# PEER layer: one-hot rows made on ScalarE, and all u blocks ahead of the first v block

## The chip, the cores and the metric

The kernel runs on one core of one Trainium2 chip. The metric is the device time of one execution in microseconds. Engines are named as the profile names them: PE is TensorE, DVE is VectorE, ACT is ScalarE, POOL is GpSimd, SP is SyncE, whose queue issues the loads.

## What is computed

The reference is a model of three layers over 256 tokens of width 1024. The change lies in one part of the first layer, a PEER layer: 16384 experts, laid out as 128 x 128, of which each token uses 8 x 16 = 128.

```
q = (xt @ w_q).reshape(BLOCK, PEER_HEADS, PEER_QDIM)
s1, s2 = q[..., :half] . keys1,  q[..., half:] . keys2
t1, i1 = top_k(s1, 16);  t2, i2 = top_k(s2, 16)
ts, sel = top_k(t1[:, None] + t2[None, :], 16)     # 16 of 256 pairs per head
idx = i1 * 128 + i2 of the pairs chosen
g = softmax(ts)
act = gelu(u[idx] . xt)
out = sum over chosen experts of (g * act) * v[idx]
```

The kernel gathers no rows of u or v. It computes GELU(u . x) for all 16384 experts and all 256 tokens, multiplies it with a matrix of coefficients that is g at the chosen experts and 0 elsewhere, and multiplies the product with all of v.

## The kernel before

Weights come as blocks of 128 x 1024 float32 (512 KB). For each block, SP issues a load into one of a few places (`prefetch`, L152), ACT makes the rounded upper part (L138), and DVE the remainder (L163, `losplits`); then the place is free for another load. `pump` runs this ahead of PE: the split on ACT is issued three blocks ahead of the block that PE works on, and DVE's part of a block one block later. The order on every engine is the order in which the program issues; nothing reorders it later. Waits between engines follow from tiles being written and read.

The experts are cut in 128 u blocks and 128 v blocks. A u block (`ublock`) is 24 matmuls of 256 columns (`lin_b`, L192 to L194), and its GELU is put into `ring`, which is 128 blocks x 256 tokens in SBUF. A v block (`row_a`, L204 to L208) is 12 matmuls of 512 columns that add into four PSUM banks.

The layer has three stretches. In the first, 66 u blocks are computed while DVE and POOL work out the top 16 (`unit`). The second builds the coefficients. `rT` holds, with heads and choices along the partitions and tokens along the columns, i1 (row 0), i2 (row 1) and g (row 2); it is filled by transposes on PE and ACT copies (L955). For every group of four tokens (64 groups, `group`) there are two factors per token, made by `onehots`: `e`, on POOL (L968), one-hot rows of i2, and `a`, on DVE (L970), one-hot rows of i1 times g. Four matmuls (L980, each two PE instructions) contract the two over the 128 choices, which gives the 128 x 128 coefficients of a token. For blocks whose GELU is already in the ring, DVE multiplies it by them (L983); for the others ACT stores the coefficients in the ring (L984), and the block's own GELU is multiplied in later (`ublock`, L901, L903, L905: columns of the tokens already built are handled apart from the rest). `e` has three buffers and `a` two; the one-hots of a group are issued one group ahead, inside the group before.

Beside the groups run u blocks: 26 of them, with `NU2 = 28` and two more ahead of the transposes. The loop issues one u block, then as many groups as keep the two lists in step:

```
for i in range(2, NU2):
    ublock(u)
    u += 1
    while g * (NU2 - 2) < NG * (i - 1):
        group(g, u)
        g += 1
```

In the third stretch the v blocks run. `coef` splits two ring blocks into upper part and remainder (L221, L222), one pair ahead. The 34 u blocks that are left are issued one behind each of the first 34 v blocks. `plan_peer` puts the loads in the same order. While the coefficients are built, three 512 KB places take incoming blocks: two of the base pool and the first half of `h`. The second half holds `rT` and becomes a fourth place when the stage ends; two pieces of the ring are added from v block 32 on.

Of the kernel before, what the change touches and what calls it, by code (L numbers as in the profile page):

```python
# [11 lines left out]
AF = mybir.ActivationFunctionType  # L12
OP = mybir.AluOpType
# [6 lines left out]
S = 256  # L20
# [5 lines left out]
NF = FF // 128  # L26
EXP_BLOCKS = 128
NU1 = 66
NU2 = 28
PACE = 1.7  # L30
QB = 6
BURST = 1.4
# [56 lines left out]
class Net:  # L89
# [665 lines left out]
    def plan_peer(self):  # L755
# [5 lines left out]
        for hd in range(8):  # L761
            p.append(A["peer_wq"][2 * hd])
            p.append(A["peer_wq"][2 * hd + 1])
            for _ in range(QB):
                p.append(A["peer_u"][u])
                u += 1
        while u < NU1 + NU2:
            p.append(A["peer_u"][u])
# [7 lines left out]
    def peer(self, h, dg, spool):  # L776
# [3 lines left out]
        nc, tc, A = self.nc, self.tc, self.A  # L780
        mm = nc.tensor.matmul
        with ExitStack() as ctx:
            one = ctx.enter_context(tc.tile_pool(name="p1", bufs=1))
            wctx = ctx.enter_context(ExitStack())
            ring = one.tile([128, EXP_BLOCKS, S], F32, name="ring")
# [26 lines left out]
            iota = self.c("iota")  # L812
# [73 lines left out]
            def ublock(b):  # L886

                n = 4 * built[0]
                if b < NU1 + 2:
                    if b % 2 == 0:  # L890
                        pair["p"] = self.ps.tile([128, 512], F32, name="b", tag="b")
                    p = pair["p"]
                    self.lin_b(p[:, (b % 2) * S:(b % 2 + 1) * S], self.chunk(), 0, x2T, KB, 0, S)
                    if b % 2 == 1:
                        nc.scalar.activation(ring[:, b - 1:b + 1, :].rearrange("p a b -> p (a b)"), p,
                                             AF.Gelu_apprx_tanh)
                    return
                p = self.bank(S)
                self.lin_b(p, self.chunk(), 0, x2T, KB, 0, S)
                if n:  # L900
                    nc.scalar.activation(p[:, :n], p[:, :n], AF.Gelu_apprx_tanh)  # L901
                if n < S:
                    nc.scalar.activation(ring[:, b, n:], p[:, n:], AF.Gelu_apprx_tanh)  # L903
                if n:
                    nc.vector.tensor_mul(out=ring[:, b, :n], in0=p[:, :n], in1=ring[:, b, :n])  # L905
# [44 lines left out]
            rT = h[:, 1, :768].rearrange("p (a b) -> p a b", b=S)  # L950
            for c0, n in ((0, 2), (2, 1)):
                p = self.ps.tile([128, 512], F32, name="acc", tag="acc")
                for i in range(2 * n):
                    nc.tensor.transpose(p[:, i * 128:(i + 1) * 128], res[:, c0 + i // 2, i % 2, :], self.ident)
                nc.scalar.activation(rT[:, c0:c0 + n, :].rearrange("p a b -> p (a b)"), p[:, :n * S], AF.Copy)  # L955

            used[1] = 0
            et = [carve((4, 128), F32, 1) for _ in range(3)]
# [3 lines left out]
            def onehots(g):  # L962
                if g >= NG:
                    return
                t0 = 4 * g
                e, a = et[g % 3], at[g % 2]
                for i in range(4):
                    nc.gpsimd.tensor_scalar(e[:, i, :], iota, rT[:, 1, t0 + i:t0 + i + 1], None, op0=OP.is_equal)  # L968
                for i in range(4):
                    nc.vector.tensor_scalar(a[:, i, :], iota, rT[:, 0, t0 + i:t0 + i + 1], rT[:, 2, t0 + i:t0 + i + 1],  # L970
                                            op0=OP.is_equal, op1=OP.mult)
                st[g] = (e, a)

            def group(g, nb):

                t0 = 4 * g
                e, a = st.pop(g)
                p = self.ps.tile([128, 512], F32, name="acc", tag="acc")
                for i in range(4):
                    mm(p[:, i * 128:(i + 1) * 128], e[:, i, :], a[:, i, :], start=True, stop=True)  # L980
                pg = p.rearrange("p (t b) -> p b t", b=128)
                onehots(g + 1)
                nc.vector.tensor_mul(out=ring[:, :nb, t0:t0 + 4], in0=pg[:, :nb, :], in1=ring[:, :nb, t0:t0 + 4])  # L983
                nc.scalar.activation(ring[:, nb:, t0:t0 + 4], pg[:, nb:, :], AF.Copy)  # L984
                built[0] = g + 1

            onehots(0)
            g = 0
            for i in range(2, NU2):
                ublock(u)  # L990
# [4 lines that stand above are left out]
# [36 lines left out]
            for i, w in enumerate(self.chunks(3)):  # L1031
                b = EXP_BLOCKS - 3 + i
# [516 lines left out]
```

## Time and profile before

Three runs took 2177.15, 2177.68 and 2179.26 us; the median is 2177.68. The profiled execution took 2177.61 us, its span is 2175.8 us.

| engine | busy us | share of the span | instructions |
|---|---|---|---|
| PE (matmul) | 2122.0 | 98% | 14386 |
| DVE | 1349.3 | 62% | 2458 |
| ACT | 1078.1 | 50% | 1720 |
| POOL | 309.7 | 14% | 436 |

The share of busy time is a mean over stretches with different limits. The chain that ended last is followed back from the last instruction; for each moment it names the work that everything behind it waited for. A row of the grouped instructions ends with the idle time of the engine just before them and what ended it. A PE instruction's time includes a tail that overlaps with the next one, so sums of PE's rows are longer than the time they cover, and starts are compared instead.

### The profile page before, as it was taken

The page shows a single profiled execution, that of the slowest core. Times are in us where ns is not written, and L with a number is a line of the kernel's source. Part 1 is how long each engine was busy: PE and PEld are TensorE (multiplying, and loading weights), DVE is VectorE, ACT ScalarE, POOL GpSimd, SP SyncE. Part 2 cuts the span into 40 slices and gives each one's busy share as a digit, 9 for nine tenths or more (in the row PEclk, how much of TensorE's full clock was granted, in tenths as well). Part 3 has the DMA queues.
Part 4 walks back from the last instruction along what each step waited for, and adds up shares of the span by engine and source line. Part 5 has one row for each costly group of instructions (what it writes and reads, how often), then busy time and mean ns, then how long its engine had stood idle before and what let it go on. Part 6 is the DMA issues. An engine that isn't in the chain of part 4 may idle for free.

```text
span 2175.8 us, 36723 instructions
## 1 busy us (share of the span) xinstructions
PE 2122.0 (98%) x14386; PEld 1914.6 (88%) x14386; DVE 1349.3 (62%) x2458; ACT 1078.1 (50%) x1720; POOL 309.7 (14%) x436
## 2 busy tenths in 40 slices
PE   8999999999998999999999999999999999999998
PEld 8987889999887889888888899887999999878997
DVE  6666669897777555555555554577554654586454
ACT  5666554444333444444445544586444544475443
POOL 1221111111999300000001000011000000010000
PEclk9999999999999999999999999999999999999999
DMA  6433455565222455555555655533555555534553
GB/s 220 144 109 107 147 176 178 181 185 175 88 79 78 148 189 196 188 187 186 193 188 170 226 183 195 166 107 130 196 179 191 168 179 197 176 98 157 198 179 117
DMA packets 99709, 356.40 MB, mean 164 GB/s; under 512 B 11040, under 2 KB 13344, under 8 KB 99280
## 3 DMA queue, kind: packets, MB, share of 16 engines
q1 hardware_dynamic: 98304, 349.58, 48.9%
q0 software_dynamic: 656, 3.41, 0.4%
q8 instruction: 114, 1.87, 0.3%
q10 hardware_dynamic: 576, 1.06, 0.1%
q14 instruction: 59, 0.48, 0.1%
HBM read 351.90 MB, written 2.10 MB: 163 GB/s over the span
## 4 chain that ended last, share of the span: by engine, by line
PE 82%; POOL 9%; DVE 5%; issue 2%; ACT 2%; DMA 0%; SPq 0%; POOLq 0%; DVEq 0%; ACTq 0%
PE b L192 15%; PE b L194 15%; PE b L193 15%; PE acc L204 10%; PE acc L206 10%; PE acc L208 10%; POOL work L968 8%; DVE wlo L163 2%; PE acc L235 1%; PE acc L237 1%; PE acc L236 1%; PE acc L299 1%; PE acc L676 0%; PE acc L677 0%; PE b L505 0%
## 5 line engine op out<-in xcount | busy, mean ns | idle before, releaser
L192 PE MATMUL b<-xhi,whi 128*128 128x256 f32 x2416 | 681.5, 282 | 2.7 <-issue 2.3
L194 PE MATMUL b<-xhi,wlo 128*128 128x256 f32 x2416 | 676.2, 280 | 2.0 <-DVE wlo L163 2.0
L193 PE MATMUL b<-xlo,whi 128*128 128x256 f32 x2416 | 676.0, 280 | 0.0
L163 DVE TENSOR_TENSOR wlo<-raw,whi 128x1024 fp32r<-128x1024 f32 x451 | 537.4, 1227 | 44.9 <-ACT whi L138 43.2
L138 ACT ACTIVATE whi<-raw 128x1024 fp32r<-128x1024 f32 x451 | 463.8, 1052 | 73.0 <-PE acc L208 43.6
L192 PEld LDWEIGHTS b<-xhi,whi 128*128 128x128 f32 x2416 | 456.0, 189 | 8.0 <-issue 2.5
L193 PEld LDWEIGHTS b<-xlo,whi 128*128 128x128 f32 x2416 | 455.9, 189 | 4.3
L194 PEld LDWEIGHTS b<-xhi,wlo 128*128 128x128 f32 x2416 | 455.8, 189 | 2.6 <-DVE wlo L163 2.6
L1101 DVE TENSOR_TENSOR silu<-silu,b 128x256 f32<-128x256 f32 x88 | 37.0, 421 | 300.9 <-PE b L194 292.4
L968 POOL TENSOR_SCALAR work<-cst,h 128x128 f32<-128x128 f32 x256 | 175.4, 706 | 23.1 <-ACT h L955 23.1
L138 ACT ACTIVATE whi<-ring 128x1024 fp32r<-128x1024 f32 x106 | 112.0, 1058 | 114.6 <-issue 43.3
L204 PE MATMUL acc<-whi,chi 128*128 128x512 f32 x500 | 157.9, 397 | 1.5 <-ACT chi L221 1.5
L206 PE MATMUL acc<-wlo,chi 128*128 128x512 f32 x500 | 157.3, 396 | 0.0
L208 PE MATMUL acc<-whi,clo 128*128 128x512 f32 x500 | 157.3, 397 | 0.0
L221 ACT ACTIVATE fhi<-silu 128x256 fp32r<-128x256 f32 x88 | 36.8, 418 | 240.8 <-DVE silu L1101 240.8
L163 DVE TENSOR_TENSOR wlo<-ring,whi 128x1024 fp32r<-128x1024 f32 x106 | 132.0, 1246 | 12.9 <-ACT whi L138 12.8
L163 DVE TENSOR_TENSOR wlo<-h,whi 128x1024 fp32r<-128x1024 f32 x103 | 126.9, 1232 | 7.6 <-ACT whi L138 7.6
L242 POOL TENSOR_SCALAR r<-ss 128x1 f32<-128x1 f32 x16 | 4.8, 298 | 864.4 <-ACT acc L269 672.6
L222 DVE TENSOR_TENSOR clo<-ring,chi 128x512 fp32r<-128x512 f32 x64 | 44.2, 693 | 120.8 <-ACT chi L221 118.9
L206 PEld LDWEIGHTS acc<-wlo,chi 128*128 128x128 f32 x500 | 94.3, 189 | 22.8
L208 PEld LDWEIGHTS acc<-whi,clo 128*128 128x128 f32 x500 | 94.2, 188 | 22.8
L192 PE MATMUL b<-ohi,whi 128*128 128x256 f32 x400 | 112.4, 281 | 0.0
(398 smaller groups left out, 3677.0 us busy)
## 6 DMA issues: line engine op xcount, KB each, us to landing
raw<-ffn_in SPq DMA_DIRECT2D x176, 512.0 KB, 4.1
raw<-ffn_out SPq DMA_DIRECT2D x88, 512.0 KB, 4.6
h<-peer_u SPq DMA_DIRECT2D x61, 512.0 KB, 4.5
ring<-peer_u SPq DMA_DIRECT2D x46, 512.0 KB, 3.7
ring<-peer_v SPq DMA_DIRECT2D x46, 512.0 KB, 3.5
h<-peer_v SPq DMA_DIRECT2D x42, 512.0 KB, 4.5
raw<-peer_v SPq DMA_DIRECT2D x40, 512.0 KB, 3.6
raw<-w_in SPq DMA_DIRECT2D x38, 512.0 KB, 4.1
```

Of the source, the lines that this page charges most:

```text
L138: nc.scalar.activation(t, self.raw[j], AF.Copy)
L163: self.nc.vector.tensor_sub(out=t, in0=self.raw.pop(j), in1=self.hi[j].bitcast(F32))
L192: mm(ps, whi[:, s], xhi[:, k, n0:n1], start=(k == 0), stop=False)
L193: mm(ps, whi[:, s], xlo[:, k, n0:n1], start=False, stop=False)
L194: mm(ps, wlo[:, s], xhi[:, k, n0:n1], start=False, stop=(k == nk - 1))
L204: mm(acc[tb * 2 + h], xhi[:, k, t], whi[:, h * 512:(h + 1) * 512], start=first, stop=False)
L206: mm(acc[tb * 2 + h], xhi[:, k, t], wlo[:, h * 512:(h + 1) * 512], start=False, stop=False)
L208: mm(acc[tb * 2 + h], xlo[:, k, t], whi[:, h * 512:(h + 1) * 512], start=False, stop=last)
L221: nc.scalar.activation(hi, src, AF.Copy)
L222: nc.vector.tensor_sub(out=lo, in0=src, in1=hi.bitcast(F32))
L968: nc.gpsimd.tensor_scalar(e[:, i, :], iota, rT[:, 1, t0 + i:t0 + i + 1], None, op0=OP.is_equal)
L1101: nc.vector.tensor_mul(out=s, in0=s, in1=pu)
```

## The change

`onehots` makes `e` on ACT. For each of four tokens one activation computes |column - i2|, with -i2 as the bias per partition, and one more over all four computes relu(1 - that). `rT` therefore holds -i2 in row 1, and its filling is three copies in place of two. `onehots` runs two groups ahead instead of one, with one more call before the loop. `NU2` is 62: 60 u blocks run beside the groups, and no u block is left for the v stretch. The ACT store behind the multiplication is left out where all blocks are already in the ring.

```diff
-NU2 = 28
+NU2 = 62
...
-                nc.scalar.activation(rT[:, c0:c0 + n, :].rearrange("p a b -> p (a b)"), p[:, :n * S], AF.Copy)
+                if c0 == 0:
+                    nc.scalar.activation(rT[:, 0, :], p[:, :S], AF.Copy)
+                    nc.scalar.activation(rT[:, 1, :], p[:, S:], AF.Copy, scale=-1.0)
+                else:
+                    nc.scalar.activation(rT[:, 2, :], p[:, :S], AF.Copy)
...
                 for i in range(4):
-                    nc.gpsimd.tensor_scalar(e[:, i, :], iota, rT[:, 1, t0 + i:t0 + i + 1], None, op0=OP.is_equal)
+                    nc.scalar.activation(e[:, i, :], iota, AF.Abs, bias=rT[:, 1, t0 + i:t0 + i + 1])
+                nc.scalar.activation(e, e, AF.Relu, scale=-1.0, bias=1.0)
...
-                onehots(g + 1)
+                onehots(g + 2)
                 nc.vector.tensor_mul(out=ring[:, :nb, t0:t0 + 4], in0=pg[:, :nb, :], in1=ring[:, :nb, t0:t0 + 4])
-                nc.scalar.activation(ring[:, nb:, t0:t0 + 4], pg[:, nb:, :], AF.Copy)
+                if nb < EXP_BLOCKS:
+                    nc.scalar.activation(ring[:, nb:, t0:t0 + 4], pg[:, nb:, :], AF.Copy)
                 built[0] = g + 1
 
             onehots(0)
+            onehots(1)
```

## Rows read from the trace of the kernel before

**Rows 1.** The page's fourth part: shares of the chain that ended last, by engine.
```profile
PE 82%; POOL 9%; DVE 5%; issue 2%; ACT 2%; DMA 0%; SPq 0%; POOLq 0%; DVEq 0%; ACTq 0%
```
**Rows 2.** Busy times by stretch: length, PE, PEld, DVE, ACT, POOL (instructions), clock, DMA.
```profile
304.00:514.00 210.00, 206.23 (x1746) 204.28 (x1747) 192.83 (x548) 98.56 (x121) 34.57 (x30) 1.00 0.59 180
549.00:726.20 177.20, 157.99 (x1131) 140.80 (x1129) 136.52 (x372) 60.07 (x143) 175.16 (x256) 0.99 0.27 84
726.20:1177.40 451.20, 451.20 (x2335) 381.78 (x2336) 242.75 (x262) 212.82 (x260) 1.67 (x3) 1.00 0.57 189
```
**Rows 3.** The chain inside 549 to 727 us: start, length, work.
```profile
548.80 163.97 POOL work L968 x240
```
**Rows 4.** Instructions grouped by line, 549 to 725 us: busy, mean ns, idle before.
```profile
L968 POOL TENSOR_SCALAR work<-cst,h 128x128 f32<-128x128 f32 x256 | 175.4, 706 | 23.1 <-ACT h L955 23.1
L980 PE MATMUL acc<-work 128*128 128x128 f32 x512 | 89.5, 301 | 17.7 <-DVE work L970 12.0 <-POOL work L968 2.5 <-ACT ring L984 0.2
...
L163 DVE TENSOR_TENSOR wlo<-raw,whi 128x1024 fp32r<-128x1024 f32 x17 | 20.8, 1224 | 0.0
```
**Rows 5.** PE in order of time, 547 to 727 us: start, length, instruction.
```profile
547.99 0.37 PE L192 MATMUL b<-xhi,whi 128*128 128x256 f32 x1
...
643.98 0.37 PE L192 MATMUL b<-xhi,whi 128*128 128x256 f32 x1
...
646.87 1.05 PE L980 MATMUL acc<-work 128*128 128x128 f32 x8
...
726.17 1.22 PE L204 MATMUL acc<-whi,chi 128*128 128x512 f32 x2 [1.48 <-ACT chi L221]
```
**Rows 6.** ACT's instructions grouped by line and shape, whole span.
```profile
L1314 ACT ACTIVATE z<-z,swmx 128x128 f32<-128x128 f32 x16 | 6.3, 395 | 11.2 <-DVE swmx L1312 11.1
...
L543 ACT ACTIVATE gel<-gel 128x512 f32<-128x512 f32 x1 | 0.6, 632 | 0.0
```
**Rows 7.** ACT in order of time, 1450 to 1454 us (a later layer).
```profile
1450.84 1.28 ACT L1161 ACT_TABLE_LOAD   x1
1452.14 0.53 ACT L1161 ACTIVATE e<-e 128x384 f32<-128x384 f32 x1
1452.57 0.48 ACT L1158 ACTIVATE e<-acc 128x384 f32<-128x384 f32 x1
1453.08 0.53 ACT L1161 ACTIVATE e<-e 128x384 f32<-128x384 f32 x1
```
**Rows 8.** ACT in order of time, 1464 to 1467 us.
```profile
1464.61 1.77 ACT L1167 ACTIVATE e<-e 128x384 f32<-128x384 f32 x4
1466.28 0.47 ACT L1158 ACTIVATE e<-acc 128x384 f32<-128x384 f32 x1
```
**Rows 9.** ACT and DVE in order of time, 633 to 638 us.
```profile
633.32 0.26 ACT L901 ACTIVATE b<-b 128x120 f32<-128x120 f32 x1 [0.35 <-PE b L194]
...
633.92 0.28 DVE L905 TENSOR_TENSOR ring<-b,ring 128x120 f32<-128x120 f32 x1 [1.13 <-ACT ring L903]
634.12 1.30 DVE L970 TENSOR_SCALAR work<-cst,h 128x128 f32<-128x128 f32 x4
635.34 0.48 DVE L983 TENSOR_TENSOR ring<-acc,ring 128x324 f32<-128x324 f32 x1
635.85 0.33 ACT L984 ACTIVATE ring<-acc 128x188 f32<-128x188 f32 x1 [1.96 <-DVE ring L983]
...
637.33 0.33 ACT L984 ACTIVATE ring<-acc 128x188 f32<-128x188 f32 x1 [1.15 <-DVE ring L983]
637.56 1.05 ACT L138 ACTIVATE whi<-raw 128x1024 fp32r<-128x1024 f32 x1
```
**Rows 10.** PE in order of time, 960 to 963 us, v blocks alone.
```profile
960.17 0.63 PE L204 MATMUL acc<-whi,chi 128*128 128x512 f32 x2
...
962.97 0.40 PE L204 MATMUL acc<-whi,chi 128*128 128x512 f32 x1
```
**Rows 11.** Loads, 726 to 960 us: count, size, median us to landing.
```profile
h<-peer_u SPq DMA_DIRECT2D x31, 512.0 KB, 4.6
```

## The prediction

> **What bounds the kernel now.** I read the page's chain that ended last first: PE holds 82% of it and POOL 9% [rows 1]. So there is a place where POOL, not PE, sets the pace. The busy times by stretch say where: in 549.0 to 726.2 us, the stage that builds the coefficients, POOL is busy 175.16 of 177.20 us, PE 157.99, DVE 136.52 and ACT only 60.07; in the stretch behind it, 726.2 to 1177.4, PE is busy for the whole 451.20 [rows 2]. The chain inside the stage is one piece: 163.97 us of POOL work of line 968 [rows 3]. The grouped instructions name it: 256 comparisons of 128x128, mean 706 ns, 4 to each of the 64 groups of tokens, and PE's matmuls of line 980 are the ones that stand idle before them [rows 4].
>
> How much of the stage PE needs is worked out from its starts. A u block starts at 643.98 and the group behind it at 646.87, so a block takes 2.89 us [rows 5]. A group is 8 PE instructions in 1.05 us, whose last, of about 0.275, overlaps with what follows: (1.05 - 0.275) / 7 = 0.11 from start to start, and 8 x 0.11 = 0.89 us [rows 5]. The stage lasts from the start of its first u block, 547.99, to the first v matmul, 726.17: 178.2 us [rows 5]. It holds 26 u blocks and 64 groups, 26 x 2.89 + 64 x 0.89 = 75.1 + 57.0 = 132.1. PE is therefore held up for 46.1 us, 1.48 of them at the end, where it waits for the first coefficients. That is what is to be had.
>
> **The change part by part.** *POOL's comparisons* go: 256 x 706 ns, and the pace of 2.7 us per group with them. Nothing else in the stage runs on POOL.
>
> *ACT's part.* Each group gets four Abs with a bias read per partition, and one Relu over 4 x 128. The nearest row for Abs is the exponential of 128x128 with such a bias, 395 ns; for Relu the 128x512 activation in place, 632 ns; its constant bias of 1.0 adds nothing visible: line 1167 has one too, and four of its instructions over 384 columns take 1.77 us, (1.77 + 3 x 0.10) / 4 = 0.52 each, as the 0.53 of line 1161 without one [rows 6, 7, 8]. Independent ACT instructions overlap by 0.10 us (1452.14 + 0.53 against the start at 1452.57), while one that reads the result of the one before starts 0.03 us after its end (1452.57 + 0.48, next at 1453.08) [rows 7]. So Abs and Relu take 3 x 0.295 + 0.395 + 0.03 + 0.632 = 1.94 us, 1.84 if the first overlaps too. If nothing overlaps it is 4 x 0.395 + 0.03 + 0.632 = 2.24; this is the upper bound, the lower is 1.84, and I take 1.84, since the rows of this engine with such a bias overlap as well.
>
> *The chain of one block.* ACT's order per block is: split of a weight block, GELU in two pieces, Abs and Relu for two groups ahead, and the copy of line 984, which waits for DVE's line 983. From the trace, with the two pieces of GELU starting at 633.32, line 905 starts at 633.92, line 970 at 634.12, line 983 at 635.34, the copy at 635.85: 2.53 us [rows 9]. ACT's own way to that point is about 0.57 of GELU and 1.84, 2.41, so the copy still waits for DVE, not for the new work. Line 983 grows from 4 x 69 to 4 x 128 columns; over its 324 columns in 0.48 us the mean of 394 is worth about 0.07 more. From the copy to the split is 0.23 us (637.33 to 637.56), on average about 0.17, since the copy shrinks to nothing; the split is 1.05, less 0.10 of overlap [rows 9]. One block: 2.53 + 0.07 + 0.17 + 0.95 = 3.72 us on ACT. Sixty blocks carry 64 groups, so four blocks have a second one, for which ACT needs 1.84 + 0.27 = 2.1: 60 x 3.72 + 4 x 2.1 = 231.6 us. PE needs 60 x 2.89 + 64 x 0.89 = 173.4 + 57.0 = 230.4 us. The two come out level. ACT, with 60.07 of 177.20 us busy, is the cover for this edit; after it there is none left.
>
> *What two level engines lose.* They wait for each other a little. The nearest stretch with a second engine almost full is 304 to 514, where DVE is busy 192.83 of 210.00 us and PE 206.23, a loss of 1.8% [rows 2]. I take 4 us of 232. Abs is issued two groups ahead (hence onehots(1) before the loop) and the splits three blocks ahead, so the four double blocks are absorbed rather than paid one by one. Before the loop ACT has 2 x 1.94 us of one-hots ahead of its first split, and the second group comes about 1 us late for PE; that is within the 4.
>
> *DVE.* The new wait is that the four comparisons of line 970 for group g+2 use the buffer that group g's matmuls read, so they wait for PE. Behind them in DVE's queue stands line 983 of group g, which waits for the same matmuls: what moves is its order, 1.1 us later, and that is in the chain above. Per block DVE has 1.22 for a remainder [rows 4], 0.28 for line 905 and 64/60 times the 1.7 from line 970's start to line 983's end [rows 9]: 3.3 us, under 3.8.
>
> *34 u blocks move* from among the v blocks into the stage, with their loads, splits, GELUs and multiplications; nothing of it is added or saved. A v block alone takes 2.80 us (960.17 to 962.97) [rows 10]. Behind the stage 128 x 2.80 = 358.4 us are left of 451.2, so 92.8 go and 34 x 2.89 = 98.3 come in the stage, already counted there. ACT's copy of the transposed indices becomes three instructions in place of two, 0.3 us once, at the head of ACT's queue. The scale of -1 costs nothing.
>
> *Loads.* SP's queue keeps its order. In the stage three 512 KB places hold incoming blocks, as before, but a block is wanted every 3.8 us in place of 6.8. From one split to the next split out of the same place there are 3 x 3.8 = 11.4 us; needed are one block until DVE's turn (3.8), its 1.22 [rows 4], and a landing, which took 4.6 us in the busier stretch behind the stage: 9.7 [rows 11]. Hidden, with 1.7 us to spare. In the v stretch four places give 4 x 2.8 = 11.2 against 2.8 + 1.22 + 4.6 = 8.6.
>
> **Sum.** Before: 178.2 + 92.8 = 271.0 us for what moves or changes. After: 230.4 + 4 + 1.5 (the same wait for the first coefficients) = 235.9. Gain 35.1. The profiled execution took 2177.61 us (span 2175.8), within 0.1 of the median 2177.68: 2177.6 - 35.1 = 2142.5, say 2143. Without any loss between ACT and PE it would be 231.9 and 2138.5; if a u block in the denser stage packed like 2.80 us, 5 less, 2133. That is the low end.
>
> **The rivals.**
>
> *ACT becomes the bound.* For: its sum is already 231.6. If nothing on it overlaps, a block takes 0.60 + 2.24 + 0.03 + 0.27 + 1.05 + 0.03 = 4.22 us and a second group 2.55: 60 x 4.22 + 4 x 2.55 + 1.5 = 264.9, a gain of 6, 2171.5. Against: the overlap in [rows 7], and DVE's waits, not ACT's work, end the copy's wait. Halfway, 4.0 us, gives 60 x 4.0 + 4 x 2.3 + 1.5 = 250.7, a gain of 20, 2157.
>
> *Loads come late.* If landing took 7 us in place of 4.6, the three places would set 12.0 / 3 = 4.0 us per block: 60 x 4.0 + 4 x 0.89 + 1.5 = 245, a gain of 26, 2152. Against: the landing in [rows 11].
>
> *Table loads; this is the slower side.* GELU, Abs and Relu run on one engine in turn. If Abs and Relu weren't served by the table that GELU has loaded, each block would load twice, and the row has 1.28 us for one, with the next instruction 0.02 us behind it [rows 7]. On a chain that has nothing to spare: 60 x (3.72 + 2.57) + 4 x 2.1 + 1.5 = 387, against 271: 116 slower, 2294. It decides from 0.63 us per block on, since 60 x 4.35 + 8.4 + 1.5 = 271. Against: line 1158's Abs runs right behind the logarithm of line 1167 with no load [rows 8], and it is the exponential of line 1161 that loads one; line 1158 at 1452.57 also follows an exponential without one [rows 7]. No row shows Relu, nor Abs behind GELU.
>
> The Trainium skill, "ScalarE: Activation LUTs", section "Table sets: the hidden batching unit", says that cheap functions such as relu and abs are filler in every set; by that rule the rival falls. The page's section "What ACT_TABLE_LOAD costs" speaks of about 1380 ns of drain on top of a 1283 ns load; by it the rival would be 60 x 2 x 1.38 = 166 us worse still. The trace has the 1283, and no such drain between its instructions.
>
> **How the numbers follow.** Likeliest, PE and ACT level: 0.65, own range 2134 to 2151. ACT bound, 2151 to 2172: 0.21. Loads, 2148 to 2160: 0.06. Table loads: 0.03. Something unseen that eats most of the gain, or more: 0.05. The range 2134 to 2164 leaves out about 2 in 10: the upper part of the second case and the last two. A measurement of this kernel tells some 0.2%, 4.4 us. Slower: 0.03 + 0.01 = 0.04; within 0.2%: 0.03; faster: 0.93.
>
> **What would show it.** POOL gone from the chain of the stage; the stage about 236 us long with 60 u blocks; PE's idle time there under 6 us; ACT over 90% busy in it; the four Abs starting about 0.30 us apart; the copy of line 984 still waiting for DVE; v blocks every 2.80 us behind it. It is wrong if ACT loads tables in the stage, if Abs starts 0.4 us apart, if PE waits for Relu block after block, or if the splits wait for loads.

## The result, and the profile after

Four runs of the changed kernel took 2129.17 to 2131.19 us, median 2129.88; the kernel before has 2177.41 over its four. The ratio is 0.9783, 95% interval 0.9771 to 0.9796: 2.2% faster. The sign and the mechanism are as forecast, but the gain is 47.5 us where 35 were forecast, and the time lies below the range. The profiled execution took 2129.37 us, its span is 2127.6.

The page's chain that ended last has lost POOL (9% in [rows 1]); PE has its share:

```profile
PE 91%; DVE 5%; ACT 2%; issue 1%; POOL 1%; DMA 0%; SPq 0%; POOLq 0%; DVEq 0%; ACTq 0%
```

Busy times by stretch, columns as in [rows 2]. The stage now runs from 547.3 to 776.2 us. In its middle PE is busy for all of 213.50 us and ACT for 203.57; POOL does nothing. What PE loses lies in the first and the last 8 us:

```profile
546.70:554.70 8.00, 7.34 (x62) 7.07 (x61) 6.17 (x20) 7.83 (x22) 0.00 (x0) 1.00 0.60 197
554.70:768.20 213.50, 213.50 (x1853) 213.50 (x1852) 169.52 (x411) 203.57 (x535) 0.00 (x0) 1.00 0.45 139
768.20:776.20 8.00, 5.66 (x51) 5.47 (x49) 6.17 (x13) 5.42 (x15) 0.00 (x0) 1.00 0.53 166
```

The waits of PE's matmuls in the stage (who waited for whom: us in total, times, longest). In [rows 4] matmuls of the groups stood idle for 17.7 us; now one of them waits, and the first v block waits for the first coefficients:

```profile
PE acc L204 <- ACT chi L221: 2.3, 1, 2.3
PE acc L986 <- ACT work L974: 0.7, 1, 0.7
```

PE in order of time, to set beside [rows 5] (the group is now line 986). From one group to the next are 3.70 us, 0.81 from the group's start to the u block and 2.89 back to a group:

```profile
641.73 1.05 PE L986 MATMUL acc<-work 128*128 128x128 f32 x8
642.54 0.36 PE L192 MATMUL b<-xhi,whi 128*128 128x256 f32 x1
...
645.43 1.05 PE L986 MATMUL acc<-work 128*128 128x128 f32 x8
```

ACT over the same block, to set beside [rows 9] (973 is Abs, 974 Relu, 991 the copy), with DVE's multiplication, line 989, that the copy waits for: no table load in it, Abs about 0.3 us apart, everything on ACT seemingly back to back:

```profile
641.93 0.24 ACT L901 ACTIVATE b<-b 128x104 f32<-128x104 f32 x1
642.20 0.30 ACT L903 ACTIVATE ring<-b 128x152 f32<-128x152 f32 x1
642.40 1.27 ACT L973 ACTIVATE work<-cst,h 128x128 f32<-128x128 f32 x4
643.70 0.64 ACT L974 ACTIVATE work<-work 128x512 f32<-128x512 f32 x1
643.74 0.54 DVE L989 TENSOR_TENSOR ring<-acc,ring 128x372 f32<-128x372 f32 x1
644.37 0.29 ACT L991 ACTIVATE ring<-acc 128x140 f32<-128x140 f32 x1
644.56 1.05 ACT L138 ACTIVATE whi<-raw 128x1024 fp32r<-128x1024 f32 x1
645.62 0.24 ACT L901 ACTIVATE b<-b 128x108 f32<-128x108 f32 x1
```

The copy starts 0.09 us after the multiplication ends (643.74 + 0.54 against 644.37). It does so, with the same 0.09, in every block with one group from 588 to 770 us: the copy still waits for DVE, as forecast. The view of waits lists only the later of these blocks, from 694 us on, where ACT was idle for 0.15 us or more; it puts 16 down to DVE and 6 to PE. The columns that DVE multiplies grow from block to block, so ACT's time from one GELU (line 901) to the next grows too, from 3.49 us early to 3.75 at the end:

```profile
763.65 0.36 ACT L901 ACTIVATE b<-b 128x240 f32<-128x240 f32 x1
...
765.61 0.67 DVE L989 TENSOR_TENSOR ring<-acc,ring 128x500 f32<-128x500 f32 x1
766.38 0.18 ACT L991 ACTIVATE ring<-acc 128x12 f32<-128x12 f32 x1 [0.32 <-DVE ring L989]
...
767.41 0.36 ACT L901 ACTIVATE b<-b 128x244 f32<-128x244 f32 x1
```

Where the 48 us of span went, from the starts of the first u block of the stage, the first v matmul, the last matmul of line 208, and the end:

| stretch | before | after | difference |
|---|---|---|---|
| ahead of the stage | 548.0 | 547.3 | -0.7 |
| the stage (26 or 60 u blocks, 64 groups) | 178.2 | 228.9 | +50.7 |
| v blocks (with 34 u blocks or none) | 446.6 | 349.9 | -96.7 |
| behind them | 1003.0 | 1001.5 | -1.5 |

The last row of the table has no cause in the change that I can show; all profiles below but two have 1001.5 to 1001.8 there, those two 1002.1 and 1003.2.

### The profile page after: what moved, and what is told of

It is laid out like the page before. It is cut to its first block, busy times and chain, and to the rows that moved or that the text cites. A ratio compares the mean times of both kernels' runs of the same rounds, so it can differ in the third digit from the quotient of the medians.

```text
span 2127.6 us, 36652 instructions
## 1 busy us (share of the span) xinstructions
PE 2091.6 (98%) x14386; PEld 1902.9 (89%) x14386; DVE 1341.4 (63%) x2458; ACT 1187.8 (56%) x2074; POOL 134.2 (6%) x180
## 4 chain that ended last, share of the span: by engine, by line
PE 91%; DVE 5%; ACT 2%; issue 1%; POOL 1%; DMA 0%; SPq 0%; POOLq 0%; DVEq 0%; ACTq 0%
PE b L192 17%; PE b L194 16%; PE b L193 16%; PE acc L204 10%; PE acc L206 10%; PE acc L208 10%; PE acc L986 2%; DVE wlo L163 1%; PE acc L235 1%; PE acc L237 1%; PE acc L236 1%; PE acc L299 1%; PE acc L676 0%; PE acc L677 0%; PE b L505 0%
## 5 line engine op out<-in xcount | busy, mean ns | idle before, releaser
L163 DVE TENSOR_TENSOR wlo<-raw,whi 128x1024 fp32r<-128x1024 f32 x458 | 545.9, 1227 | 45.0 <-ACT whi L138 43.3
L138 ACT ACTIVATE whi<-raw 128x1024 fp32r<-128x1024 f32 x458 | 470.7, 1051 | 48.7 <-PE acc L208 20.4
L138 ACT ACTIVATE whi<-h 128x1024 fp32r<-128x1024 f32 x97 | 102.1, 1053 | 47.9 <-PE acc L208 26.7
L163 DVE TENSOR_TENSOR wlo<-h,whi 128x1024 fp32r<-128x1024 f32 x97 | 119.7, 1234 | 7.6 <-ACT whi L138 7.6
L204 PEld LDWEIGHTS acc<-whi,chi 128*128 128x128 f32 x500 | 93.9, 188 | 25.0 <-ACT chi L221 2.5
```

Of the source, the lines that this page charges most:

```text
L138: nc.scalar.activation(t, self.raw[j], AF.Copy)
L163: self.nc.vector.tensor_sub(out=t, in0=self.raw.pop(j), in1=self.hi[j].bitcast(F32))
L204: mm(acc[tb * 2 + h], xhi[:, k, t], whi[:, h * 512:(h + 1) * 512], start=first, stop=False)
```

## The experiments

All twelve were compared with the kernel before on their own chip (2177.1 to 2177.3 there). "Stage" and "v" are the stretches of the table, from each kernel's profile; the stage here counts from the transposes of line 954, 0.6 us earlier.

| kernel | median us | ratio to before, 95% | stage | v |
|---|---|---|---|---|
| changed | 2129.88 | 0.9771 to 0.9796 | 229.5 | 349.9 |
| changed, again | 2130.80 | 0.9771 to 0.9804 | 229.5 | 351.4 |
| one-hots on ACT, 26 u blocks | 2175.33 | 0.9983 to 1.0002 | 176.7 | 446.6 |
| one-hots on ACT, 43 u blocks | 2149.53 | 0.9855 to 0.9888 | 200.7 | 399.0 |
| one-hots on ACT, 54 u blocks | 2136.38 | 0.9796 to 0.9828 | 218.8 | 368.0 |
| one-hots on POOL, 60 u blocks | 2136.68 | 0.9801 to 0.9834 | 232.9 | 352.0 |
| Relu's part on POOL | 2134.48 | 0.9787 to 0.9820 | 232.1 | 351.4 |
| a fifth Abs | 2132.86 | 0.9779 to 0.9812 | 231.3 | 352.4 |
| a fifth and sixth Abs | 2155.94 | 0.9887 to 0.9920 | 254.2 | 352.3 |
| last u block moved | 2127.08, 2127.55 | 0.9755 to 0.9789 | 227.4 | 349.9 |
| the same, one-hots on POOL | 2134.34 | 0.9789 to 0.9822 | 232.2 | 351.4 |
| last u block moved, groups later | 2126.81 | 0.9753 to 0.9785 | 226.7 | 349.9 |

**Each part alone.** The first kernel undoes the order and keeps ACT, the second keeps the order and undoes ACT.

```diff
-NU2 = 62
+NU2 = 28
```

> The changed kernel with the one-hots on ACT, but only 26 u blocks beside the 64 groups, as before. Theory A (the two parts pay only together: POOL's pace was dear because 2.5 groups stood beside each u block, and ACT is no faster there): ACT has 26 x 1.55 us of splits and GELUs and 64 x 2.15 us of Abs, Relu and copy, 178 us, what the stage took before; 2177 within 6. Theory B (POOL itself was the cost, and to leave it is the gain): PE needs 26 x 2.80 + 64 x 0.89 = 130 us, the stage is 48 shorter, about 2130; at least half of that gain, 2153 or less.

```diff
-    nc.scalar.activation(e[:, i, :], iota, AF.Abs, bias=rT[:, 1, t0 + i:t0 + i + 1])
-nc.scalar.activation(e, e, AF.Relu, scale=-1.0, bias=1.0)
+    nc.gpsimd.tensor_scalar(e[:, i, :], iota, rT[:, 1, t0 + i:t0 + i + 1], None, op0=OP.is_equal)
```

> The changed kernel with all 60 u blocks beside the groups, but the one-hots of i2 on POOL by comparison, two groups ahead. Theory A: POOL needs 64 x 2.4 to 2.8 = 154 to 180 us, under the 226 of PE, so it is hidden; 2130 within 3, and perhaps 1 us less than the changed kernel since ACT is free at the end of the stage. Theory B: POOL's part is still the bound or slows DVE, and most of the gain is gone: 2150 or more.

ACT alone gains nothing that can be told: 2175.33, ratio 0.9993. The stage takes 176.7 us, and by the busy times of that kernel ACT has simply taken POOL's place (169.07 of 176.60 us busy):

```profile
547.00:723.60 176.60, 145.26 (x1144) 140.99 (x1142) 129.03 (x373) 169.07 (x467) 0.00 (x0) 0.94 0.27 85
```

Its waits of PE in the stage, where matmuls and weight loads stand behind Relu:

```profile
PEld acc L986 <- ACT work L974: 33.1, 21, 2.5
PE acc L986 <- ACT work L974: 20.4, 17, 2.3
```

The order alone gains 40 of the 47 us. Theory B falls, but for a small part: POOL does slow DVE, by about 0.1 us per block. Theory A holds for both, but POOL is 6 us behind the changed kernel and not level with it, so the 2130 that I expected was missed. The waits of the kernel with POOL, of PE and then of ACT, show why:

```profile
PE acc L204 <- ACT chi L221: 4.5, 1, 4.5
...
ACT ring L990 <- DVE ring L988: 101.1, 52, 2.3
```

With POOL, ACT has nothing to do between GELU and the copy (line 990), and waits there for DVE in nearly every block. In the changed kernel Abs and Relu fill most of that wait (4.5 us in 16 blocks are listed), but the copy is released by DVE there too. What differs is the time that DVE takes: from its four comparisons (line 975 here, 976 in the changed kernel) to its multiplication 1.09 to 1.15 us beside POOL, 1.02 in the changed kernel. From GELU to GELU it is 3.73 us in the mean of the 54 blocks with one group, against 3.63 in the changed kernel and 3.69 on PE. So ACT falls behind PE, and the first coefficients come 4.5 us late, not 2.3.

**How much room ACT has.** Three kernels change ACT's load.

```diff
+nc.scalar.activation(spare, iota, AF.Abs, bias=rT[:, 1, t0:t0 + 1])
 nc.scalar.activation(e, e, AF.Relu, scale=-1.0, bias=1.0)
```

> The changed kernel with a fifth Abs of 128x128 per group on ACT into a tile that nobody reads, 0.295 us each, 64 x 0.295 = 18.9 us. If ACT and PE are level (ACT's own chain is 3.67 us per block against 3.70 on PE): 15 to 19 us slower than the changed kernel, 2145 to 2149. If ACT has slack that the trace doesn't show: under 5 us, 2130 to 2135.

It is 2 to 3 us slower than the two runs of the changed kernel, not 15 to 19: ACT had room, though the trace of the changed kernel shows it back to back. In this kernel's trace ACT takes 3.58 us for a block with five Abs (644.54 to 648.12), and PE keeps its 3.69:

```profile
643.59 1.05 ACT L138 ACTIVATE whi<-raw 128x1024 fp32r<-128x1024 f32 x1
644.54 0.25 ACT L901 ACTIVATE b<-b 128x104 f32<-128x104 f32 x1
...
646.19 0.39 ACT L975 ACTIVATE spare<-cst,h 128x128 f32<-128x128 f32 x1
646.48 0.62 ACT L976 ACTIVATE work<-work 128x512 f32<-128x512 f32 x1
647.00 0.27 ACT L993 ACTIVATE ring<-acc 128x140 f32<-128x140 f32 x1
...
648.12 0.26 ACT L901 ACTIVATE b<-b 128x108 f32<-128x108 f32 x1
```

The room is in the overlaps. Here GELU starts 0.10 us before the split ends, and the copy 0.10 before Relu ends; in the changed kernel both start 0.01 to 0.03 after. An ACT instruction that has to wait gives up its overlap with the one ahead, and the profile counts no idle time for it. GELU waits there for PE, the copy for DVE, and the fifth Abs runs inside the copy's wait: from GELU to GELU a block with one group takes 3.65 us in the mean between 668 and 720 us and 3.73 behind that, with five Abs as with four. The Trainium skill, "ScalarE: Activation LUTs", section "What ACT_TABLE_LOAD costs", says that back-to-back ACTIVATEs overlap by about 93 ns; the trace agrees where nothing is waited for, and shows no overlap where something is. Its section "Table sets: the hidden batching unit", with relu and abs in every set, agrees with the trace as well: no load stands in the stage beside GELU.

```diff
+for _ in range(2):
+    nc.scalar.activation(spare, iota, AF.Abs, bias=rT[:, 1, t0:t0 + 1])
 nc.scalar.activation(e, e, AF.Relu, scale=-1.0, bias=1.0)
```

> The changed kernel with two more Abs of 128x128 per group on ACT into a tile that nobody reads. With one more, ACT packed a block into 3.58 us and PE kept its 3.69. If ACT's room is the difference between 3.69 and its own 3.29: six take 3.87 us a block and PE follows, 60 x 0.18 and some 3 us at the double blocks and the end, 2142 to 2147. If ACT still has room: 2132 to 2135.

With two more, PE does follow ACT, which takes 3.98 us per block, not the 3.87 expected (the two Abs, into one tile, take 0.74 to Relu's start, not 0.59):

```profile
702.15 0.29 ACT L901 ACTIVATE b<-b 128x152 f32<-128x152 f32 x1
...
703.79 0.83 ACT L976 ACTIVATE spare<-cst,h 128x128 f32<-128x128 f32 x2
704.53 0.62 ACT L977 ACTIVATE work<-work 128x512 f32<-128x512 f32 x1
...
706.13 0.29 ACT L901 ACTIVATE b<-b 128x156 f32<-128x156 f32 x1
```

The time, 2155.94, is 9 us above the range that I expected. 60 x 0.11 is 6.6 of it; the rest is not separated.

```diff
-nc.scalar.activation(e, e, AF.Relu, scale=-1.0, bias=1.0)
+nc.gpsimd.tensor_scalar(e, e, 0.0, None, op0=OP.is_equal)
```

> The changed kernel, with |column - i2| on ACT as there, and the Relu replaced by one comparison with zero on POOL over 4 x 128, which takes 0.65 us per group off ACT. Theory A1 (PE alone sets the stage's 229 us, ACT only matters at its end): 2129 to 2130, at most 1.5 us less. Theory A2 (ACT, back to back at 3.69 us per block, holds PE back): down to PE's own 60 x 2.80 + 64 x 0.89 = 225 us, 2126.

Less work on ACT made it slower, by some 4 us: neither theory expected that. At the start of the stage PE waits twice for POOL, 1.9 us in all in place of 0.7, and its granted clock is 0.50 behind that, from 553.6 to 557.0 us; together that is about the 2.6 us by which the stage is longer. The v stretch is 1.5 us longer, as in the second run of the changed kernel, and the profile has 1.7 us behind the v blocks, without a cause that I can show. Nothing is won against this, since the copy on ACT still waits for DVE (40.1 us in 56 blocks): from GELU to GELU a block takes 3.65 us between 668 and 720 us and 3.73 behind that, as with Relu on ACT. ACT's own load is not what sets the stage, as A1 had it.

**How many u blocks it takes.**

```diff
-NU2 = 62
+NU2 = 45
```

> The changed kernel with 43 u blocks beside the 64 groups and 17 among the v blocks. From the kernel with 26 u blocks, ACT takes 2.04 us per group and 1.42 per block when it never waits: 43 x 1.42 + 64 x 2.04 = 192 us, PE 43 x 2.80 + 64 x 0.89 = 177. If the engine with the larger sum sets the stage: 14 to 20 us slower than the changed kernel, 2145 to 2151. If PE does even here: 2130 to 2133.

2149.53, as the larger sum had it; PE waits 20 times for Relu (12.9 us). Where the two sums are equal:

```diff
-NU2 = 62
+NU2 = 56
```

> The changed kernel with 54 u blocks beside the groups and 6 among the v blocks. ACT 54 x 1.42 + 64 x 2.04 = 207 us, PE 54 x 2.80 + 64 x 0.89 = 208: the two sums are equal here. If level engines lose something to each other, as the prediction had it with 4 us: 2133 to 2137. If they lose nothing: 2130 to 2132.

2136.38, some 6 us slower than with 60. The waits of PE in this kernel: seven times for Relu, 3.7 us, and 3.6 at the end:

```profile
PE acc L986 <- ACT work L974: 3.7, 7, 0.9
PE acc L204 <- ACT chi L221: 3.6, 1, 3.6
```

That is not yet a loss of level engines, since the sums leave out the copy's wait for DVE. With it a block with one group takes ACT 3.62 us in the mean here, and one of the ten with two groups 5.60: 44 x 3.62 + 10 x 5.60 = 215 us beside PE's 208, and the stage took 218.2 from its first u block. ACT's chain is the longer one. At 60 u blocks the same count gives 56 x 3.63 + 4 x 5.58 = 225.6 us beside 225.3 on PE, and the stage took 228.9.

**What is left in the stage.** The changed kernel was run again beside the next ones:

> The changed kernel again, on the chip of the next three, to compare them with: 2130 within 2.

```diff
-NU2 = 62
+NU2 = 61
...
-        while u < NU1 + NU2:
+        while u < NU1 + NU2 + 1:
...
             coef(0)
+            ublock(u)
+            u += 1
```

> The changed kernel with the last u block taken out of the stage and put behind the split of the first coefficients, ahead of the first v block, so that PE has 2.8 us of work while it would wait for them. If PE's 2.3 us of waiting at the end, and the lower clock that follows it in some runs, are what is left in the stage: 2 to 4 us less than the changed kernel. If that block's own GELU and splits only push the wait into the first v blocks: no difference, within 1 us.

> The kernel with the last u block behind the first coefficients, again, to compare the next three with: 2127 within 2.

2127.08 against 2130.80: 3.7 us less, and 2127.55 on another chip. The wait of 2.3 us is down to 0.4. The rest is the clock. The changed kernel's repeat waited as long as the first run (2.4 us), and its granted clock in the first 4 us of v blocks was near half, 1.2 of 2.4 GHz, where the first run's was full. Windows of the repeat:

```profile
774.40:776.80 2.40, 0.03 (x1) 0.00 (x0) 1.18 (x4) 1.28 (x5) 0.00 (x0) 1.00 0.63 157
776.80:778.80 2.00, 1.99 (x6) 1.57 (x7) 2.00 (x3) 1.43 (x2) 0.00 (x0) 0.63 1.05 424
778.80:780.80 2.00, 2.00 (x6) 1.59 (x5) 1.56 (x2) 0.00 (x0) 0.00 (x0) 0.52 0.29 43
```

Windows of the profile after, at the same place:

```profile
773.80:776.20 2.40, 0.06 (x2) 0.02 (x1) 1.17 (x4) 1.28 (x5) 0.00 (x0) 1.00 0.54 167
776.20:778.20 2.00, 2.00 (x9) 1.64 (x10) 2.00 (x3) 1.40 (x2) 0.00 (x0) 1.00 0.94 383
```

Its v stretch is 1.5 us longer for it (351.4 against 349.9). The first run is the exception: in eleven of the profiles PE stood idle for 1.5 to 4.7 us ahead of the first v block, the kernel before among them, and ten of these have a granted clock of 0.50 to 0.73 over the next 2 us. With the last u block moved, PE waits 0.4 us or less, and the clock stays at 1.00 in both profiles.

```diff
-                while g * (NU2 - 2) < NG * (i - 1):
+                while (g + 1) * (NU2 - 2) <= NG * (i - 1):
```

> The same, with the groups spread so that the first u block of the stage has one group behind it and not two. If PE's 0.7 us of waiting for the second group's Relu is a loss of its own: 0.5 to 1.5 us less than the kernel above. If the wait is filled elsewhere: no difference that can be told, within 1 us.

This takes the 0.7 us of waiting for the second group away as well (stage 226.7, PE busy 226.30 of 226.60 us). Its 2126.81 beside 2127.55 is the difference expected, but too small for their intervals to tell apart. Both are faster than the kernel before and than the changed one.

> The same move of the last u block, with the one-hots of i2 on POOL. If the engine that makes them doesn't matter once 60 u blocks stand beside 64 groups, and the 6 us that POOL was behind came from the longer wait at the end (4.5 us) and the clock after it: within 1.5 us of the kernel above with ACT. If POOL slows DVE or holds PE back in the stage itself: 3 us or more behind it.

POOL stays 7 us behind ACT (2134.34): the move alone doesn't close it. PE still waits 2.2 us for the first coefficients, since ACT comes there late. It waits 1.1 at the start and has a granted clock of 0.50 behind that (555 to 558 us), and the v stretch again has the lower clock (351.4). So with 60 u blocks beside the groups the engine that makes the one-hots matters, by a seventh of the gain.

## Why the prediction was right and wrong

*The bound, and what is to be had: right.* PE was held up by POOL's pace (48 us, counted as in the next paragraph, where the prediction had 46.1), and neither part alone takes all of that: ACT alone nothing, the order alone 40 us, both 47. The prediction treated the two parts as one edit and named ACT as the cover; it did not say that POOL itself would nearly fit beside 60 u blocks, though [rows 4] give it: 256 x 0.706 = 181 us, under PE's 225.

*PE's sum: the step that failed first.* 2.89 us for a u block runs up to the first matmul of the group, and holds some 0.09 us of the changeover; 0.89 for a group, worked out from its own starts, holds it again. Measured from group to group it is 3.70, not 3.78: 60 x 3.695 + 4 x 0.89 = 225.3 where the prediction had 230.4. That is 5.1 us. The text had 2.80 as its low end, which is the right term beside 0.89; the time it gave, 2133, lay just outside the range that was stated, and the measured time is 3 us below it.

*What two level engines lose: wrong here, by 2 us.* 4 us and a wait of 1.5 at the end were taken; the profile has 2.3 at the end, 1.3 by difference at the start (228.9 - 225.3 - 2.3), and nothing between: 3.6 in place of 5.5. The chain was right: the copy waits for DVE. ACT and PE are level, as forecast, but at 225 us and not at 231. ACT's 3.72 per block was read along DVE's lines 970 and 983 as POOL slowed them: from line 905 to DVE's multiplication it was 1.42 us in [rows 9] and is 1.21 without POOL (642.53 to 643.74). Measured it is 3.49 to 3.75, 3.63 in the mean, which includes blocks where ACT follows PE at 3.69. After a block with two groups ACT is about 1 us behind, and the splits and one-hots issued ahead cover that; it catches up over the blocks that take it less than 3.69. Behind the last block with two groups, at 721 us, it doesn't: the blocks take 3.70 to 3.75 there. This late lag fits the longer wait at the end, 2.3 in place of 1.5; no run separates it.

*34 u blocks move: mis-sized by 3.9 us.* 128 whole v blocks of 2.80 were taken from a stretch that I had ended at 1177.4, inside the last blocks. From the first v matmul to the last of line 208 it is 96.7 us, not 92.8: 34 x 2.80 = 95.2, and some 1.5 for the low clock that the kernel before has at the head of its v blocks (0.50 granted from 726.2 to 728.2 us) and the profile after has not. These 1.5 are luck of that execution.

*Sum.* 35.1 + 7.0 in the stage + 3.9 + 0.7 ahead and 1.5 behind, which no step foresaw, make 48.2, the difference of the profiled runs.

*The rivals.* Table loads: none. Loads late: the middle of the stage has no wait for them. ACT as the bound: at 60 u blocks it is level with PE and costs little; at 54 and below, and at 60 with six Abs, it is the bound.

## What to carry to other kernels

Where one engine makes small operands for PE, divide both engines' sums by the stretch that they share: here PE had 34 blocks elsewhere that needed nothing from the slow engine, and laying them beside it was worth 40 us, while a change of engine alone was worth nothing that can be told. Measure a period of the bound engine from one start to the next start of the same kind; two pieces measured to different edges count the changeover twice. And an engine that looks back to back may be following another: load it a little and see whether the time moves. Look, too, for the instruction that always starts the same time after another engine's end: it is released there, though no idle time is listed.

## What the runs showed of the hardware

An ACT instruction that has to wait, or reads what the one ahead wrote, loses about 0.1 us of overlap, which is not listed as idle time: blocks of 3.65 to 3.73 us held room for a fifth Abs of 0.3. POOL at work slows DVE's small comparisons of 128x128: 363 to 366 ns in the mean in the kernels with the one-hots on POOL, 338 to 343 with all of them on ACT. And of two executions with the same 2.4 us in which PE stood idle at the end of the stage, one ran its next 4 us at about half clock and lost 1.5 us, the other did not; of eleven profiles with 1.5 us or more of that idle time, ten show the lower clock.
